# Cross attention with cached keys turned by VectorE's block transpose, and the prompt's keys asked for one head ahead

## The chip, the cores and the metric

The kernel runs on one core of one Trainium2 chip. The metric is the device time of one execution in microseconds. Three runs of the kernel before gave 2087.58, 2092.14 and 2093.4 us (median 2092.14).

## The reference

A two-layer encoder step in fp32 over a prompt of 512 frames and 8 running streams of 16 frames each ("sample"). Each layer is a mixer, a cross attention and a feed-forward block. The change is in the cross attention: 4 heads of 256 dimensions over 256 memory tokens. The sample's keys and values come from a cache, for each stream its own; the prompt's are projected from its memory.

```python
def cross_attn(h, mk, mv, w_q, w_o):
    b, t, _ = h.shape
    q = (h @ w_q).reshape(b, t, X_HEADS, X_HEAD_DIM)
    s = jnp.einsum('bqhd,bkhd->bhqk', q, mk).astype(jnp.float32) * X_SCALE
    p = jax.nn.softmax(s, axis=-1).astype(mv.dtype)
    o = jnp.einsum('bhqk,bkhd->bqhd', p, mv).reshape(b, t, X_WIDTH)
    return o @ w_o

# in the trunk, for each layer i
x = x + cross_attn(rmsnorm(x, g_cross[i]), mem_k[i], mem_v[i], w_x_q[i], w_x_o[i])
```

## The kernel before

The program runs the first mixer (FoX), cross attention, feed-forward, the second mixer (MLA), cross attention and feed-forward, one after the other. Activations lie transposed (features on partitions) as a pair of rounded value and rest, `hT0` and `hT1` (four tiles), for 640 columns: 512 of the prompt and 128 of the sample. A product of two such pairs is three matmuls (hi by hi, hi by lo, lo by hi); weights are loaded as `raw`, ScalarE casts the rounded part `whi` (L150) and VectorE subtracts for the rest `wlo` (L151). `gemm` accumulates in a PSUM tile `mm`; all these matmuls have line L204, and those of the prompt's attention (`mm3`) L218. `evac_split` evicts a PSUM tile as such a pair: ScalarE first (L222, L225 with a scale), then VectorE (L223, L226).

`cross_phase` (L828) does one cross attention. Its parts:

- `q_list(h)`: the query projection of head h, two blocks of 128 dimensions (`dt`) by two halves of 320 columns. The weight's 128 columns are the stationary operand. The prompt's queries go to `qT0`, `qT1`, the sample's, spread over 32-column blocks, to `Qp`.
- `sample_list(pr, bq)`: for a pair of heads and four streams. `keys` loads a key `kr` (128 tokens on partitions, 2 token blocks, 256 dimensions; L941, three keys ahead, four buffers), turns it with four TensorE transposes into PSUM (L956) and copies it to `KT`, on VectorE for even streams (L960), on ScalarE for odd ones (L962). `scores` (L969) fills one PSUM tile for four streams with matmuls of 32 columns, then comes the softmax (reduction L872, exponential L874, reciprocal L344, scaling L345), `trans` (L978, copied to `PTs` by ScalarE, L980), `values` (L992) and `turn` (L1002, to `oTs`).
- `prompt_list(h)`: `load` asks for `kv`, the head's keys and values, from a DRAM buffer; `keys` turns them on TensorE (L891) to `kT0`, `kT1` and casts the values to `v0`, `v1` (one buffer each); then, for two halves of the queries, scores, transposes (L915) and values to `oT0`, `oT1`.
- `out_steps(h)`: the output projection of a head, added to `X` in place by VectorE (L332).

`merge` interleaves three lists evenly, and there are four merges per layer: sample (0,0) with prompt head 0 and the query projection of head 2; sample (0,1) with prompt 1 and q 3; sample (1,0) with prompt 2 and the output of head 0; sample (1,1) with prompt 3 and the output of head 1. The program below is not executed in the written order: a list scheduler puts each engine's instructions in one static order, in which the engine then runs them; all loads of the phase are issued by SyncE's queue in its own such order. The merges of layer 0 lie from about 555 to 681 us, those of layer 1 start near 1499 us.

## Time and profile before

| what | us |
|---|---|
| runs of the kernel before | 2087.58, 2092.14, 2093.4 |
| median | 2092.14 |
| the profiled execution | 2091.71 |
| its span in the trace | 2089.9 |
| TensorE busy in the span | 2034.7 |
| VectorE busy | 1390.8 |
| ScalarE busy | 888.0 |

The span is the profiled execution as the trace has it; 1.8 us of the time lie outside. Busy time of TensorE counts matmuls, whose ends are modelled, so the start of one instruction to the start of the next is the better measure of what an instruction takes up. Loads of stationary operands (PEld) overlap matmuls.

### The profile page before, as it was taken

The page shows a single profiled execution, that of the slowest core. Times are in us where ns is not written, and L with a number is a line of the kernel's source. Part 1 is how long each engine was busy: PE and PEld are TensorE (multiplying, and loading weights), DVE is VectorE, ACT ScalarE, POOL GpSimd, SP SyncE. Part 2 cuts the span into 40 slices and gives each one's busy share as a digit, 9 for nine tenths or more (in the row PEclk, how much of TensorE's full clock was granted, in tenths as well). Part 3 has the DMA queues.
Part 4 walks back from the last instruction along what each step waited for, and adds up shares of the span by engine and source line. Part 5 has one row for each costly group of instructions (what it writes and reads, how often), then busy time and mean ns, then how long its engine had stood idle before and what let it go on. Part 6 is the DMA issues. An engine that isn't in the chain of part 4 may idle for free. (4 is left out here: it accounts for less than half of the span.)

```text
span 2089.9 us, 34810 instructions
## 1 busy us (share of the span) xinstructions
PE 2034.7 (97%) x13629; PEld 1817.9 (87%) x13629; DVE 1390.8 (67%) x2658; ACT 888.0 (42%) x1723; POOL 195.2 (9%) x398
## 2 busy tenths in 40 slices
PE   7999999999999999999999989999999999999998
PEld 7988888777987899999998978887987899999996
DVE  5455555655556896687677567777556896686686
ACT  4434444544443443343344455554443443343342
POOL 1222222210000000000002301101000000000000
PEclk9999999999999999999999999999999999999999
DMA  7565655477464322232222342113463322232221
GB/s 194 119 160 124 148 135 142 146 243 229 151 197 133 100 88 74 81 91 71 81 82 64 96 109 52 53 51 102 149 196 131 101 81 75 80 99 71 81 81 61
DMA packets 334203, 236.37 MB, mean 113 GB/s; under 512 B 99140, under 2 KB 298564, under 8 KB 334040
## 3 DMA queue, kind: packets, MB, share of 16 engines
q1 hardware_dynamic: 334040, 234.15, 38.8%
q8 instruction: 108, 1.77, 0.4%
q14 instruction: 55, 0.45, 0.1%
HBM read 216.90 MB, written 17.21 MB: 112 GB/s over the span
## 5 line engine op out<-in xcount | busy, mean ns | idle before, releaser
L204 PE MATMUL mm<-hT,whi 128*128 128x320 f32 x1744 | 287.5, 311 | 2.9 <-ACT hT L222 2.9
L151 DVE TENSOR_TENSOR wlo<-raw,whi 128x1024 fp32r<-128x1024 f32 (+4 forms) x145 | 169.8, 1174 | 156.5 <-ACT whi L150 116.5
L204 PEld LDWEIGHTS mm<-hT,whi 128*128 128x128 f32 x1744 | 261.0, 188 | 6.8 <-ACT hT L222 4.3
L332 DVE TENSOR_TENSOR X<-mm,X 128x512 f32<-128x512 f32 x270 | 183.5, 687 | 119.7 <-PE mm L204 118.1
L150 ACT CAST whi<-raw 128x1024 fp32r<-128x1024 f32 (+4 forms) x145 | 144.8, 1003 | 146.7 <-PE mm L204 74.9
L204 PE MATMUL mm<-whi,oT 128*128 128x512 f32 x544 | 180.3, 407 | 3.8 <-DVE X L332 2.2
L1136 ACT CAST whi<-tw 128x512 fp32r<-128x512 f32 (+1 forms) x120 | 91.9, 766 | 213.7 <-PE mm L204 127.4
L204 PE MATMUL mm<-whi,aT 128*128 128x512 f32 x560 | 173.0, 390 | 1.2 <-ACT aT L1101 1.2
L204 PE MATMUL mm<-hT,wlo 128*128 128x320 f32 x872 | 156.7, 312 | 0.0
L204 PEld LDWEIGHTS mm<-hT,wlo 128*128 128x128 f32 x872 | 133.3, 188 | 3.3 <-issue 3.2
L232 POOL TENSOR_SCALAR rstd<-ss 128x1 f32<-128x1 f32 x49 | 16.2, 330 | 1265.4 <-ACT hn L230 1261.0
L204 PE MATMUL mm<-s,whi 128*128 128x320 f32 x768 | 128.2, 309 | 0.0
L204 PE MATMUL mm<-whi,hT 128*128 128x256 f32 (+2 forms) x800 | 125.5, 295 | 0.3 <-ACT whi L150 0.3
L204 PEld LDWEIGHTS mm<-whi,aT 128*128 128x128 f32 x560 | 104.4, 188 | 23.5 <-ACT aT L1101 2.0
L204 PEld LDWEIGHTS mm<-whi,oT 128*128 128x128 f32 x544 | 96.7, 189 | 26.2 <-DVE X L332 4.6
L204 PEld LDWEIGHTS mm<-s,whi 128*128 128x128 f32 x768 | 116.6, 188 | 0.0
L1137 DVE TENSOR_TENSOR wlo<-tw,whi 128x512 fp32r<-128x512 f32 (+1 forms) x120 | 103.5, 862 | 19.1 <-ACT whi L1136 17.4
L204 PEld LDWEIGHTS mm<-whi,hT 128*128 128x128 f32 x800 | 109.1, 191 | 3.8 <-issue 1.7
L204 PE MATMUL mm<-wlo,oT 128*128 128x512 f32 x272 | 109.0, 401 | 0.0
L204 PE MATMUL mm<-wlo,aT 128*128 128x512 f32 x280 | 108.8, 389 | 0.0
L1136 ACT CAST whi<-raw 128x1024 fp32r<-128x1024 f32 x44 | 46.3, 1052 | 131.7 <-PE mm L204 71.0
L204 PE MATMUL ps_s<-whi,aT 128*128 128x512 f32 x320 | 98.6, 389 | 0.0
(336 smaller groups left out, 4199.4 us busy)
## 6 DMA issues: line engine op xcount, KB each, us to landing
rawg<-w_ffn_gu SPq DMA_DIRECT2D x80, 512.0 KB, 3.8
raw<-w_ffn_down SPq DMA_DIRECT2D x44, 512.0 KB, 3.7
raw<-w_x_kv SPq DMA_DIRECT2D x32, 512.0 KB, 4.4
kr<-cache_mem_k SPq DMA_DIRECT2D x64, 256.0 KB, 4.8
vr<-cache_mem_v SPq DMA_DIRECT2D x32, 512.0 KB, 6.1
raw<-w_fox_in SPq DMA_DIRECT2D x30, 512.0 KB, 6.5
kr<-cache_fox_k SPq DMA_DIRECT2D x64, 128.0 KB, 5.1
vr<-cache_fox_v SPq DMA_DIRECT2D x16, 512.0 KB, 5.2
```

The source lines that it names most:

```text
L150: A.copy(hi[:, 0:m], raw[:, 0:m])
L151: V.tensor_tensor(lo[:, 0:m], raw[:, 0:m], hi[:, 0:m].bitcast(F32), ALU.subtract)
L204: T.matmul(st["ps"][:, 0:n], lhsT=l, rhs=r, start=(j == 0), stop=(j == m - 1))
L232: G.tensor_scalar(r, ss, EPS, None, ALU.add)
L332: V.tensor_tensor(xs, ps, xs, ALU.add)
L1136: A.copy(hi[:, o:o + m], src)
L1137: V.tensor_tensor(lo[:, o:o + m], src, hi[:, o:o + m].bitcast(F32), ALU.subtract)
```

## The change

The cached keys are no longer turned on TensorE. Each key comes in four DMAs (`fill_keys`), 32 partitions each, one for each 64 of the 256 dimensions: 32 tokens on partitions, 8 token blocks by 64 dimensions. One VectorE instruction (`turn_keys`) turns all 32x32 blocks and writes `KT` without PSUM; it reads every second element, so that a block of 128 partitions holds the even dimensions of a head and the other the odd ones. The queries must have the same split: `q_list` loads a head's 256 weight columns at once (two units of four row blocks, instead of one unit of eight for each 128 columns) and gives TensorE the even or the odd columns as stationary operand, and the prompt's key transposes read every second column, too. The prompt's `kv` of head h+1 is asked for right after the keys of head h were turned, that of head 0 ahead of the first merge.

```diff
@@ -828,7 +828,7 @@
 
     def cross_phase(l, nx, rest):
         w_q, w_o = I["w_x_q"][l], I["w_x_o"][l]
-        mk = I["cache_mem_k"][l].rearrange("b (m p) h d -> p (b m) (h d)", p=P)
+        mk = I["cache_mem_k"][l].rearrange("b (m j) h d -> b j m (h d)", j=32)
         mv = I["cache_mem_v"][l].rearrange("b (m p) h d -> p (b m) (h d)", p=P)
         with tc.tile_pool(name=f"x{l}", bufs=2, reuse_waits="tile") as xp:
             AHEAD = 3
@@ -842,11 +842,15 @@
                 L = []
                 d = {}
 
-                def load(dt):
-                    if dt == 0:
-                        qs_[h] = [xp.tile([P, 2, NP], F32R, tag=f"qT{i}", name=f"qT{i}", bufs=2) for i in range(2)]
-                    c0 = h * XD + dt * P
-                    d[dt] = load_w([(0, P, w_q[:, c0:c0 + P])], per=8)
+                def load():
+                    qs_[h] = [xp.tile([P, 2, NP], F32R, tag=f"qT{i}", name=f"qT{i}", bufs=2) for i in range(2)]
+                    d["w"] = load_w([(0, XD, w_q[:, h * XD:(h + 1) * XD])])
+
+                def ops(dt, half):
+
+                    hs = slice(half * HALF, (half + 1) * HALF)
+                    return [(d["w"].get(wi, k).rearrange("p (n t) -> p t n", t=2)[:, dt], nx.T[ai][:, k, hs])
+                            for wi, ai in PASSES for k in range(KD)]
 
                 def done(ps, dt, half):
                     qT = qs_[h]
@@ -860,12 +864,18 @@
 
                 for half in range(2):
                     for dt in range(2):
-                        if half == 0:
-                            L.append(lambda dt=dt: load(dt))
-                        L += gemm(lambda dt=dt, half=half: ws_ops(d[dt], slice(0, P), nx.T,
-                                                                  slice(half * HALF, (half + 1) * HALF), KD),
-                                  HALF, lambda ps, dt=dt, half=half: done(ps, dt, half), parts=3)
-                return L
+                        L += gemm(lambda dt=dt, half=half: ops(dt, half), HALF,
+                                  lambda ps, dt=dt, half=half: done(ps, dt, half), parts=3)
+                return [load] + L
+
+            def fill_keys(r, src, h):
+
+                for g in range(4):
+                    c0 = h * XD + 64 * g
+                    S.dma_start(r[32 * g:32 * g + 32], src[:, :, c0:c0 + 64])
+
+            def turn_keys(dst, r):
+                V.transpose(dst, r.rearrange("p m (i t) -> p t m i", t=2))
 
             def softmax(pw, sp):
                 nm = small.tile([P, 1], F32, tag="nm", name="nm")
@@ -874,22 +884,26 @@
                 A.activation(pw, sp[:, 0:NMEM], AF.Exp, bias=nm, accum_out=ss)
                 softmax_tail(pw, ss, NMEM)
 
+            kvs = {}
+
+            def load_kv(h):
+                if h < 4:
+                    kv = npool.tile([P, 2, 2, XD], F32, tag="gb", name="kv", bufs=1)
+                    kvs[h] = [kv[:, i] for i in range(2)]
+                    for i in range(2):
+                        S.dma_start(kv[:, i], kvd[l][i].rearrange("(t p) n -> p t n", p=P)[:, :, h * XD:(h + 1) * XD])
+
             def prompt_list(h):
                 d = {}
 
-                def load():
-                    kv = npool.tile([P, 2, 2, XD], F32, tag="gb", name="kv", bufs=1)
-                    d["kv"] = [kv[:, i] for i in range(2)]
-                    for i in range(2):
-                        S.dma_start(kv[:, i], kvd[l][i].rearrange("(t p) n -> p t n", p=P)[:, :, h * XD:(h + 1) * XD])
-
                 def keys():
+                    d["kv"] = kvs.pop(h)
                     d["kT"] = [xp.tile([P, 2, NMEM], F32R, tag=f"kT{i}", name=f"kT{i}", bufs=1) for i in range(2)]
                     pt = psum_t()
                     for dt in range(2):
                         for mt in range(2):
                             T.transpose(out=pt[:, dt * NMEM + mt * P:dt * NMEM + (mt + 1) * P],
-                                        in_=d["kv"][0][:, mt, dt * P:(dt + 1) * P], identity=ident)
+                                        in_=d["kv"][0][:, mt].rearrange("p (n t) -> p t n", t=2)[:, dt], identity=ident)
                     evac_split(d["kT"][0], d["kT"][1], pt.rearrange("p (d m) -> p d m", m=NMEM))
                     d["v"] = [xp.tile([P, 2, XD], F32R, tag=f"v{i}", name=f"v{i}", bufs=1) for i in range(2)]
                     evac_split(d["v"][0], d["v"][1], d["kv"][1])
@@ -925,7 +939,7 @@
                     oc = slice(q2 * 256, (q2 + 1) * 256)
                     evac_split(oTp[h][0][:, :, oc], oTp[h][1][:, :, oc], op.rearrange("p (d q) -> p d q", q=256))
 
-                L = [load, keys]
+                L = [keys, lambda: load_kv(h + 1)]
                 for q2 in range(2):
                     L += [lambda q2=q2: scores(q2), trans, lambda q2=q2: values(q2)]
                 return L
@@ -936,9 +950,8 @@
 
                 if n < 32:
                     pr, bq, hh, b = n // 16, n // 8 % 2, n // 4 % 2, n % 4
-                    hc = slice((2 * pr + hh) * XD, (2 * pr + hh + 1) * XD)
-                    krs[n] = xp.tile([P, 2, XD], F32, tag="kr", name="kr", bufs=4)
-                    S.dma_start(krs[n], mk[:, 2 * (4 * bq + b):2 * (4 * bq + b) + 2, hc])
+                    krs[n] = xp.tile([P, 8, 64], F32, tag="kr", name="kr", bufs=4)
+                    fill_keys(krs[n], mk[4 * bq + b], 2 * pr + hh)
 
             def sample_list(pr, bq):
                 Q = Qps[pr]
@@ -947,19 +960,9 @@
                 def keys(hh, b):
                     n = 16 * pr + 8 * bq + 4 * hh + b
                     load_key(n + AHEAD)
-                    kr = krs.pop(n)
                     if b % 2 == 0:
                         d["KT"][hh, b // 2] = xp.tile([P, 2, 2, NMEM], F32, tag="KT", name="KT", bufs=4)
-                    pt = psum_t()
-                    for dt in range(2):
-                        for mt in range(2):
-                            T.transpose(out=pt[:, dt * NMEM + mt * P:dt * NMEM + (mt + 1) * P],
-                                        in_=kr[:, mt, dt * P:(dt + 1) * P], identity=ident)
-                    src = pt.rearrange("p (d m) -> p d m", m=NMEM)
-                    if b % 2 == 0:
-                        V.tensor_copy(d["KT"][hh, b // 2][:, 0], src)
-                    else:
-                        A.copy(d["KT"][hh, b // 2][:, 1], src)
+                    turn_keys(d["KT"][hh, b // 2][:, b % 2], krs.pop(n))
 
                 def scores():
                     sp = psum_s()
@@ -1030,8 +1033,9 @@
             for n in range(AHEAD):
                 load_key(n)
             ql = q_list(0)
-            for f in ql[:6] + rest[:1] + ql[6:8] + rest[1:] + ql[8:] + q_list(1):
+            for f in ql[:5] + rest[:1] + ql[5:7] + rest[1:] + ql[7:] + q_list(1):
                 f()
+            load_kv(0)
             merge(sample_list(0, 0), prompt_list(0), q_list(2))
             merge(sample_list(0, 1), prompt_list(1), q_list(3))
             merge(sample_list(1, 0), prompt_list(2), out_steps(0))
```

The scheduler's order changes with it, in the cross phases alone. The first place is the end of merge 0 on TensorE: from the last sample scores to the sample's values. `mm_6786` and `mm_6773` are the last query projection of the merge, `ps_s_6752` and `ps_s_6748` the sample's scores, `pws` its softmax, `vr` its values. The kernel before:

```order
L969 MATMUL ps_s_6752<-KT_6651,Qp0_6193 32x256 x2
L915 MATMUL ps_t_6779<-cst_79,hn_6710 128x128 x4
L204 MATMUL mm_6786<-hT00_6090,whi_6606 128x320 x4
L204 MATMUL mm_6786<-hT01_6091,whi_6606 128x320 x4
L204 MATMUL mm_6786<-hT10_6092,whi_6606 128x320 x4
L204 MATMUL mm_6786<-hT11_6093,whi_6606 128x320
L978 MATMUL ps_t_6795<-cst_79,pws_6769 128x128 x2
L204 MATMUL mm_6786<-hT11_6093,whi_6606 128x320 x3
L204 MATMUL mm_6786<-hT00_6090,wlo_6607 128x320
L992 MATMUL ps_o_6808<-vr_6611,PTs_6798 32x256 x2
```

In the changed kernel, at the same place on the same engine:

```order
L204 MATMUL mm_6773<-hT11_6093,whi_6508 128x320 x4
L204 MATMUL mm_6773<-hT00_6090,wlo_6503 128x320 x4
L204 MATMUL mm_6773<-hT01_6091,wlo_6509 128x320 x4
L972 MATMUL ps_s_6748<-KT_6664,Qp0_6193 32x256
L972 MATMUL ps_s_6748<-KT_6582,Qp0_6193 32x256 x2
L972 MATMUL ps_s_6748<-KT_6664,Qp0_6193 32x256 x2
L981 MATMUL ps_t_6791<-cst_79,pws_6765 128x128 x2
L995 MATMUL ps_o_6804<-vr_6613,PTs_6794 32x256 x2
L995 MATMUL ps_o_6804<-vr_6647,PTs_6794 32x256 x2
```

The projection's matmuls stood between the scores, the softmax's transposes (L978) and the values (L992); now they stand ahead of the last scores, and the transposes (L981) and values (L995) follow one on the other.

The second place is the border of merge 0 and merge 1 on TensorE, from the last values of the prompt (`ps_o`) on; `kr` is a cached key, `mm_6894` the next merge's projection, `kT0`, `kT1` the prompt's next keys. The kernel before:

```order
L218 MATMUL ps_o_6827<-PT0_6777,v1_6544 128x256
L204 MATMUL mm_6786<-hT01_6091,wlo_6607 128x320 x2
L1002 MATMUL ps_t_6853<-cst_79,osb_6825 128x128 x4
L956 MATMUL ps_t_6869<-cst_79,kr_6622 128x128 x4
L204 MATMUL mm_6894<-hT00_6090,whi_6878 128x320 x4
L204 MATMUL mm_6894<-hT01_6091,whi_6878 128x320 x4
L204 MATMUL mm_6894<-hT10_6092,whi_6878 128x320 x4
```

In the changed kernel, at the same place on the same engine:

```order
L218 MATMUL ps_o_6823<-PT0_6782,v1_6523 128x256
L1005 MATMUL ps_t_6849<-cst_79,osb_6821 128x128 x4
L905 MATMUL ps_t_6885<-cst_79,kv_6550 128x128 x4
L218 MATMUL ps_s_6955<-kT0_6883,qT0_6365 128x256
L218 MATMUL ps_s_6969<-kT0_6883,qT0_6365 128x256
L218 MATMUL ps_s_6955<-kT1_6884,qT0_6365 128x256
L218 MATMUL ps_s_6955<-kT0_6883,qT1_6366 128x256
```

The next projection stood behind the output's transposes (L1002) and one key; now the prompt's keys (L905) follow the output's transposes (L1005), and their scores come at once.

The third place is the same end of merge 0 on VectorE; `qT1` is the eviction of the query projection, `nm` the softmax's maximum, `KT_6664` the last pair of keys of the merge. The kernel before:

```order
L151 TENSOR_TENSOR wlo_6993<-raw_6991,whi_6992 128x1024
L872 TENSOR_REDUCE nm_6770<-ps_s_6752 128x1
L223 TENSOR_TENSOR PT1_6778<-ps_t_6779,PT0_6777 128x512
L344 RECIPROCAL rc_6774<-ssum_6772 128x1
L345 TENSOR_SCALAR pws_6769<-pws_6769,rc_6774 128x256
L151 TENSOR_TENSOR wlo_7259<-raw_7257,whi_7258 128x1024
L223 TENSOR_TENSOR oT1_6548<-ps_o_6827,oT0_6547 128x2x256
L226 SCALAR_TENSOR_TENSOR qT1_6490<-mm_6786,qT0_6489 128x192
```

In the changed kernel, at the same place on the same engine:

```order
L878 STREAM_TRANSPOSE KT_6664<-kr_6561 128x512
L223 TENSOR_TENSOR PT1_6783<-ps_t_6784,PT0_6782 128x512
L226 SCALAR_TENSOR_TENSOR qT1_6500<-mm_6773,qT0_6499 128x192
L878 STREAM_TRANSPOSE KT_6664<-kr_6577 128x512
L882 TENSOR_REDUCE nm_6766<-ps_s_6748 128x1
L344 RECIPROCAL rc_6770<-ssum_6768 128x1
L345 TENSOR_SCALAR pws_6765<-pws_6765,rc_6770 128x256
```

The eviction of the last projection (`mm_6786`) stood behind the softmax's steps; now that of `mm_6773` stands ahead of the last block transpose and the softmax's maximum.

## Rows read from the trace of the kernel before

**Rows 1.** Page, part 1: busy us, share of span, instructions.

```profile
PE 2034.7 (97%) x13629; PEld 1817.9 (87%) x13629; DVE 1390.8 (67%) x2658; ACT 888.0 (42%) x1723; POOL 195.2 (9%) x398
```

**Rows 2.** Table by stretch: length, busy us, clock, DMA share, GB/s.

```profile
616.00:651.00 35.00, 34.84 (x255) 27.90 (x255) 23.15 (x44) 13.61 (x31) 0.00 (x0) 1.00 0.59 190
```

**Rows 3.** Timeline, TensorE: start us, us, engine, line, operation.

```profile
643.71 0.41 PE L978 MATMUL ps_t<-cst,pws 128*128 128x128 f32 x2
...
644.75 1.93 PE L992 MATMUL ps_o<-vr,PTs 128*32 128x256 f32 x32
...
649.53 0.60 PE L956 MATMUL ps_t<-cst,kr 128*128 128x128 f32 x4
649.89 0.71 PE L204 MATMUL mm<-whi,oT 128*128 128x512 f32 x2
```

**Rows 4.** Groups by line, program: busy us, mean ns, idle before.

```profile
L956 PEld LDWEIGHTS ps_t<-cst,kr 128*128 128x128 f32 x256 | 30.0, 140 | 6.1 <-DMA kr<-cache_mem_k 2.2 <-ACT KT L962 1.6 <-DVE KT L960 0.4
...
L960 DVE COPY KT<-ps_t 128x512 f32<-128x512 f32 x32 | 22.0, 688 | 8.1 <-PE ps_t L956 8.1
L692 DVE STREAM_TRANSPOSE KT<-kr 128x512 f32<-128x512 f32 x32 | 21.6, 693 | 0.0
```

**Rows 5.** Groups by line, layer 0's merges (555 to 681): softmax.

```profile
L872 DVE TENSOR_REDUCE nm<-ps_s 128x1 f32<-128x256 f32 x20 | 8.5, 423 | 8.7 <-PE ps_s L218 6.5 <-PE ps_s L969 2.1
...
L344 DVE RECIPROCAL rc<-ssum 128x1 f32<-128x1 f32 x20 | 3.1, 158 | 1.2 <-ACT hn L874 1.2
...
L874 ACT ACTIVATE pws<-ps_s,nm 128x256 f32<-128x256 f32 x4 | 1.9, 481 | 0.0
...
L345 DVE TENSOR_SCALAR pws<-pws,rc 128x256 f32<-128x256 f32 x4 | 1.4, 349 | 0.1
L874 ACT ACTIVATION_READ_ACCUMULATOR pws<-ps_s,nm 128x1 f32 x4 | 0.8, 204 | 0.0
```

**Rows 6.** Groups by line, same stretch: evictions of the projections.

```profile
L332 DVE TENSOR_TENSOR X<-mm,X 128x512 f32<-128x512 f32 x21 | 14.5, 688 | 6.8 <-PE mm L204 6.6
...
L226 DVE SCALAR_TENSOR_TENSOR qT<-mm,qT 128x192 fp32r<-128x192 f32 (+1 forms) x10 | 3.8, 404 | 0.0
...
L225 ACT ACTIVATE qT<-mm 128x192 fp32r<-128x192 f32 (+1 forms) x9 | 3.2, 381 | 0.1
```

**Rows 7.** Timeline of ScalarE after a merge's last values.

```profile
649.17 0.62 ACT L222 CAST v<-kv 128x512 fp32r<-128x512 f32 x1 [1.84 <-PE ps_o L218]
649.70 0.58 ACT L222 CAST oT<-ps_o 128x512 fp32r<-128x512 f32 x1
650.17 0.27 ACT L222 CAST oTs<-ps_t 128x128 fp32r<-128x128 f32 x1
```

**Rows 8.** Groups by line, 555 to 681: the prompt's keys.

```profile
L223 DVE TENSOR_TENSOR kT<-ps_t,kT 128x512 fp32r<-128x512 f32 x4 | 2.8, 692 | 3.4 <-ACT kT L222 3.4
...
L222 ACT CAST kT<-ps_t 128x512 fp32r<-128x512 f32 x4 | 2.3, 586 | 4.5 <-PE ps_t L891 4.5
```

**Rows 9.** Groups by line, 555 to 681: idle weight loads.

```profile
L992 PEld LDWEIGHTS ps_o<-vr,PTs 128*32 128x32 f32 x128 | 3.8, 109 | 3.2 <-ACT PTs L980 1.1
...
L978 PEld LDWEIGHTS ps_t<-cst,pws 128*128 128x128 f32 x8 | 0.8, 140 | 1.4 <-PE mm L204 0.8 <-issue 0.7
```

**Rows 10.** Page, part 5: the projections' weight loads.

```profile
L204 PEld LDWEIGHTS mm<-hT,whi 128*128 128x128 f32 x1744 | 261.0, 188 | 6.8 <-ACT hT L222 4.3
```

**Rows 11.** Timeline, TensorE: a piece of the query projection.

```profile
588.04 2.15 PE L204 MATMUL mm<-hT,whi 128*128 128x320 f32 x13
```

**Rows 12.** The key tile: issues, ns min/median/max.

```profile
L941 SPq DMA_DIRECT2D kr<-cache_mem_k x64: 367/368/679, 515.2 to 1594.9; - x64
```

**Rows 13.** Page, part 6: KB each, median us to landing.

```profile
kr<-cache_mem_k SPq DMA_DIRECT2D x64, 256.0 KB, 4.8
vr<-cache_mem_v SPq DMA_DIRECT2D x32, 512.0 KB, 6.1
...
kr<-cache_fox_k SPq DMA_DIRECT2D x64, 128.0 KB, 5.1
```

## The prediction

> **What bounds the kernel now.** I read the page's busy table first. TensorE is busy in 97% of the span and VectorE in 67% [rows 1]; the next question is whether that also holds where the change acts. The change touches only the cross attention, whose work on cached keys lies in four merges per layer. The table by stretch, read for one of these merges, shows TensorE busy for 34.84 of 35 us at a granted clock of 1.00, VectorE for 23.15 us, the DMA engines at 0.59 [rows 2]. So within a merge TensorE's in-order queue sets the end: an instruction taken out of it shortens the merge by its pitch, and an instruction in it that has to wait lengthens the merge by the wait. Elsewhere the order of every engine stays as it was; there I expect no change.
>
> The timeline of TensorE shows why its queue has no holes now. The sample's two softmax transposes start at 643.71, the values that need them start at 644.75, and the copy of the transposes lies beneath projection matmuls put between the two [rows 3]. The same holds for the scores, the key evictions and the prompt's softmax: each wait has matmuls of the projection in front of it.
>
> **What the change removes.** 256 transposes leave TensorE, four per key. A key's four start at 649.53 and the next matmul starts at 649.89, 0.36 us later [rows 3], so 64 keys are worth 64 x 0.36 = 23 us. Their weight loads waited 6.1 us in the whole program, for key DMAs and key copies [rows 4]; that goes too. At the places where new waits will stand there are small waits already: weight loads of the values and of the softmax transposes sat idle for 3.2 and 1.4 us in one layer's merges [rows 9], some 5 us, or 10 for both layers; since the new waits take their place I count them as gone (bounds 0 and 10, as part of that idle time lies beside running matmuls). Together 23 + 6 + 10 = 39 us, at least 23.
>
> **VectorE.** It loses 32 copies of 0.688 us (22 us) and gains 64 block transposes. The nearest row is the first mixer's block transpose of the same size, 693 ns [rows 4], read without a step; the new one reads every second element. I take 0.69 us: 44 us, so 22 us more, 2.8 per merge. In that merge it makes 23.15 + 2.8 of 35 us: not the bound by itself. If the step doubled it, it would be 8 x 0.69 = 5.5 us per merge more, of which only the transposes at the end of a merge are waited for (below); half of that stands in the upper end.
>
> **What moves: the end of every merge.** This is the term that decides. In the new order the last projection gemm runs in one piece and the sample's tail stands behind it; nothing is left between the links. On TensorE: last gemm, last scores, the two transposes of the softmax, values of the sample, values of the prompt, transposes of the output, of the prompt's keys, and the next prompt's scores. On VectorE the last block transposes stand behind the eviction of that last gemm. Each link, per merge:
>
> (T) Last gemm to last scores. In merge 0: eviction on ScalarE about 0.34 and on VectorE 0.35 (means 0.381 and 0.404 over two widths, the last piece being the narrow one), then one block transpose of 0.69, and some 0.1 for each of three handovers: 1.7 us. In merge 1 two block transposes follow: 2.4. In merges 2 and 3 the eviction is the addition to X of 0.688 [rows 6] and two transposes follow: 2.4. Per layer 1.7 + 3 x 2.4 = 8.9.
>
> (B) Scores to softmax transposes: reduction 0.42, exponential 0.48 with its accumulator read 0.20, reciprocal 0.16, scaling 0.35 [rows 5], with handovers 0.4: 2.0 us, four times 8.0.
>
> (C) Softmax transposes to values: from 643.71 to 644.75 it takes 1.04 us [rows 3], of which the two transposes themselves are some 0.2: 0.8, four times about 3.
>
> (V) The last of the four value loads. It is issued after a key load that waits for the second-last block transpose, in merges 1 and 2. Landing takes 6.1 us [rows 13] and the work from there to its use some 5.4: 0.5 to 2.6 late; as the load's issues are spread, I take 1.0, twice: 2.
>
> (D) Before the next prompt's scores. ScalarE casts v 0.62, oT 0.58, oTs 0.27 and only then kT 0.59, all after the prompt's values end; TensorE has eight transposes, 0.8 to 0.9 us, for that time. ScalarE's starts are 0.5 apart [rows 7]: kT is there about 2.1 after the values, 1.2 after the transposes; VectorE's part, 0.69 [rows 8], then holds the third score matmul for some 0.6 more: 1.85, in merges 0, 1 and 2: 5.5.
>
> (E) The first prompt softmax and the next weights, which now arrive at the start of a merge instead of a merge ahead: a softmax of 1.6 [rows 5], less some 0.75 of scores beside it, is 0.85, three times, and 0.5 in the last, with 0.65 between the first two heads: 3.7.
>
> The sum is 8.9 + 8.0 + 3 + 2 + 5.5 + 3.7 = 31 per layer, 62 for two, against a gain of 39. Bounds: 45 if the handovers vanish and V and E are covered; 80 if V is 2.6 and each block transpose is half as long again.
>
> **Loads that move.** Each key becomes four DMAs of 32 partitions: 256 issues of 0.368 us in place of 64, 192 x 0.368 = 71 us more on the sync queue [rows 12] over eight merges, 9 per merge of some 31. Its queue has waits to spend. The first mixer loads its keys in just this form and they land in about the time of the others, 5.1 against 4.8 us [rows 13]. With three keys asked for ahead and one key used in some 3.9 us I cost this at nothing; the cover is those 11 us. The prompt's k and v load one head ahead is at nothing too: it replaces a wait that the old order already covered. The Trainium skill, "DMA: Bandwidth & Descriptors", Specifications, says that transfers below 512 B miss line rate; a key's runs here fall from 1 KB to 256 B, which speaks against this change. No run here shows runs of 256 B, and the fox keys with runs of 128 B land in 5.1 us; by the page late keys (below) would be likelier, by the row they are not.
>
> **Strided weights.** 768 projection matmuls now read their stationary operand with a step of two. Nothing in the trace does that. A contiguous load lasts 188 ns [rows 10], and 13 matmuls of 320 columns take 2.15 us with the last one's tail, some 0.15 each [rows 11], so there is little slack; at no cost 0, and at twice the pitch of the short transposes (0.36/4 = 0.09, thus 0.2 against 0.15) 768 x 0.05 = 40 us, at most 55. I take 0: loads of 188 ns at a pitch of 0.15 already overlap each other, so that a load alone doesn't set the pitch. The Trainium skill, "SBUF — State Buffer", Door 1: The DMA port swizzle, states that SBUF is read in lines of 16 bytes and that two hits in a line keep full bandwidth: a step of two fp32 still has two. No run here shows it.
>
> **The sum.** The profiled execution took 2091.7 us, 0.4 below the median of the three runs, so they stand for each other. 2091.7 - 39 + 62 = 2115. About 0.3%, 6 us, is what a measurement of this kernel can tell from no change.
>
> **Rivals.**
> - *Slower, the tails as above* (0.56): 2115, from 2098 (stalls of 45) to 2135 (stalls of 80).
> - *Faster: only the softmax is exposed* (0.13). If the chains T, D and E find their inputs earlier than I think, B and C alone remain, 2 x 11 = 22: 2091.7 - 39 + 22 = 2075, or 2065 if C is covered as well. It decides where the stalls fall below 33. For it: TensorE's 97% says that every removed instruction pays. Against it: T stands in the order, not in an estimate.
> - *No change* (0.12): T and B alone decide, 2 x 17 = 34, or the gain is only 23 with half the stalls: 2087 to 2097.
> - *Late keys* (0.12): four issues per key and four times the packets make each merge wait for one key, some 3.9 us, eight times: 2115 + 31 = 2146. For it: the DMA share of 0.59 in merges. Against it: the fox keys.
> - *Strided weight loads cost* (0.07): 2115 + 40 to 55 = 2155 to 2170.
>
> **How the numbers follow.** The likeliest gives 2115. Faster by over 0.3%: 0.13. Within: 0.12. Slower: 0.56 + 0.12 + 0.07 = 0.75. The range from 2078 to 2150 leaves out about half of the faster case, the strided loads and parts of the late keys, near 2 in 10.
>
> **What would show it.** In the profile after: TensorE's busy share in the merges falls to near 85%; idle time before the sample's scores released by VectorE's block transpose, before the softmax transposes by the scaling, before the values by ScalarE's copy, before the prompt's scores by kT, in the sizes above. The block transpose's mean should be 0.69, the pitch of the 320-column matmuls in the query projection 0.15, and key DMAs should release nearly nothing. Wrong would be: merges shorter by some 5 us each (the order's chain is then hidden), a pitch of 0.2 in the projection, or waits of TensorE or VectorE on key DMAs.

## The result, and the profile after

The changed kernel takes 2127.74 us (median of four runs, 2126.04 to 2131.19) against 2090.42 for the kernel before on the same chip: a ratio of 1.0176, 95% interval 1.0159 to 1.0193, so 37 us slower. Its profiled span is 2125.1 us. The first line of the page, to be held against [rows 1] (busy us, share of the span, instructions):

```profile
PE 2030.1 (96%) x13373; PEld 1799.3 (85%) x13373; DVE 1408.9 (66%) x2690; ACT 868.6 (41%) x1691; POOL 197.2 (9%) x398
```

TensorE has 256 matmuls fewer (its transposes count as such) and is busy for only 4.6 us less, in a span that is 35 us longer. The timeline of TensorE at the end of merge 0 shows where it stands still. Columns: start us, us, line, operation, out<-in, count, and in brackets the idle time ahead with what ended it.

```profile
576.75 1.33 PE L204 MATMUL mm<-hT,wlo 128*128 128x320 f32 x8
579.52 1.05 PE L972 MATMUL ps_s<-KT,Qp 128*32 128x256 f32 x10 [1.43 <-DVE KT L878]
582.36 0.41 PE L981 MATMUL ps_t<-cst,pws 128*128 128x128 f32 x2 [1.79 <-DVE pws L345]
583.23 3.47 PE L995 MATMUL ps_o<-vr,PTs 128*32 128x256 f32 x32 [0.46 <-ACT PTs L983]
587.42 1.71 PE L218 MATMUL ps_o<-PT,v 128*128 128x256 f32 x12 [0.71 <-ACT osb L1000]
...
590.85 0.50 PE L218 MATMUL ps_s<-kT,qT 128*128 128x256 f32 x2 [0.81 <-ACT kT L222]
591.84 1.46 PE L218 MATMUL ps_s<-kT,qT 128*128 128x256 f32 x10 [0.48 <-DVE kT L223]
...
595.50 0.30 PE L929 MATMUL ps_t<-cst,hn 128*128 128x128 f32 x1 [0.44 <-DVE hn L345]
```

Read the brackets from above: 1.43 us until the last block transpose (link T of the prediction), 1.79 until the softmax is scaled (B), 0.46 until PTs is copied (C), 0.71 until osb is copied, 0.81 and 0.48 until the prompt's keys are there (D), 0.44 for the prompt's softmax (E): 6.1 us in all, at links that had matmuls of the projections between them before (for another merge in [rows 3]). And the sample's 32 value matmuls take 3.47 us where [rows 3] has 1.93. In the other merges of the layer:

```profile
619.26 2.66 PE L995 MATMUL ps_o<-vr,PTs 128*32 128x256 f32 x32 [0.46 <-ACT PTs L983]
...
654.22 3.36 PE L995 MATMUL ps_o<-vr,PTs 128*32 128x256 f32 x32 [0.46 <-ACT PTs L983]
...
689.88 1.93 PE L995 MATMUL ps_o<-vr,PTs 128*32 128x256 f32 x32 [0.46 <-ACT PTs L983]
```

The wait for the copy is the same, the values' length is not. The table by stretch (busy us of TensorE, weight loads, VectorE, ScalarE, GpSimd; then the granted clock, the share of the DMA engines, GB/s) tells two causes apart:

```profile
583.00:587.00 4.00, 3.47 (x32) 1.39 (x32) 1.02 (x2) 0.40 (x2) 0.00 (x0) 0.57 1.05 312
619.00:622.00 3.00, 2.55 (x32) 1.04 (x32) 1.05 (x2) 0.24 (x2) 0.00 (x0) 1.00 1.08 252
654.00:658.00 4.00, 3.36 (x32) 1.65 (x32) 1.01 (x2) 0.54 (x2) 0.00 (x0) 0.58 1.03 289
...
583.23:619.26 36.03, 29.90 (x226) 24.51 (x226) 17.01 (x38) 11.10 (x28) 0.00 (x0) 0.96 0.58 148
...
1510.00:1660.00 150.00, 127.86 (x870) 100.06 (x869) 79.22 (x161) 43.51 (x103) 0.00 (x0) 0.94 0.57 151
```

In merges 0 and 2 the clock is down to 0.57 and 0.58, near the lower of TensorE's two levels (1.2 of 2.4 GHz), after waits of 1.43, 1.79 and 0.46 us within some 5 us (merge 0); in merge 1 it is 1.00 and the values are 2.66 us long all the same. The same three waits, of 1.40 to 1.43, 1.79 and 0.46 us, stand in all eight merges, and the clock fell in five of them (in layer 1 in merges 0, 1 and 3). What decides between them is not shown.

From one merge's values to the next it takes 36.0, 35.0 and 35.7 us; before, the same rows start at 582.75, 613.04, 644.75 and 674.93, 30.3, 31.7 and 30.2 apart. That is 4.8 us per merge, and the same three intervals of layer 1 give 4.9 (107.8 us in all against 93.2). Eight merges at that rate make 38 us: the loss lies in the merges. TensorE is busy for 29.90 of 36.03 us from the values of merge 0 to those of merge 1, which is 83%; near 85% was forecast.

What answers to [rows 4] and [rows 9], groups by line over the program (busy us, mean ns, idle ahead and what ended it):

```profile
L878 DVE STREAM_TRANSPOSE KT<-kr 128x512 f32<-128x512 f32 x64 | 43.0, 693 | 0.0
...
L972 PE MATMUL ps_s<-KT,Qp 128*32 128x256 f32 x256 | 25.1, 386 | 11.3 <-DVE KT L878 11.3
...
L995 PE MATMUL ps_o<-vr,PTs 128*32 128x256 f32 x256 | 23.5, 494 | 3.8 <-ACT PTs L983 3.7
```

The block transpose with a step of two takes 693 ns, as without a step, and VectorE never waited ahead of one: no key came late.

For the projections' weight loads the row of [rows 10] does not do, since most of its 1744 loads are in other phases and have no step. From 555 to 579 us they are those of the query projection, in the changed kernel and then in the kernel before:

```profile
L204 PEld LDWEIGHTS mm<-hT,whi 128*128 128x128 f32 x64 | 9.6, 196 | 0.8 <-DVE hn L345 0.4 <-issue 0.4
...
L204 PEld LDWEIGHTS mm<-hT,whi 128*128 128x128 f32 x59 | 8.7, 188 | 0.0
```

A load with a step of two takes 196 ns against 188. The pitch of the matmuls hardly moves: 8 matmuls take 1.33 us in the row of 576.75 above, 0.15 each from start to start, as in [rows 11].

### The profile page after: what moved, and what is told of

The parts are those of the page before. It is cut to its first block, busy times and chain, and to the rows that moved or that the text cites. A ratio compares the mean times of both kernels' runs of the same rounds, so it can differ in the third digit from the quotient of the medians.

```text
span 2125.1 us, 34528 instructions
## 1 busy us (share of the span) xinstructions
PE 2030.1 (96%) x13373; PEld 1799.3 (85%) x13373; DVE 1408.9 (66%) x2690; ACT 868.6 (41%) x1691; POOL 197.2 (9%) x398
```

## The experiments

The ratio of each is to the kernel before on the same chip, with its 95% interval; the changed kernel's own is 1.0176. In the edits `...` stands for lines left out.

**One DMA per key (e1).** The key loads alone are undone; all else of the change is kept. The keys' elements then lie in other places than the scores need, so this version is of use for its time alone.

```diff
-        mk = I["cache_mem_k"][l].rearrange("b (m j) h d -> b j m (h d)", j=32)
+        mk = I["cache_mem_k"][l].rearrange("b (m p) h d -> b p m (h d)", p=P)
...
-                for g in range(4):
-                    c0 = h * XD + 64 * g
-                    S.dma_start(r[32 * g:32 * g + 32], src[:, :, c0:c0 + 64])
+                S.dma_start(r.rearrange("p a b -> p (a b)").rearrange("p (m d) -> p m d", m=2), src[:, :, h * XD:(h + 1) * XD])
```

> Everything of the change but the form of the key loads: each cached key comes in one DMA of 1 KB runs instead of four of 256 B runs (the keys' elements then lie in the wrong places, so the sample's scores are not the reference's; the number and size of all VectorE and TensorE instructions stay). The scheduler then puts projection matmuls back between the sample's scores, softmax transposes and values. Theory that the order of the merge's end is the cause: the stalls vanish and the 25 us of TensorE transposes are gained, 2058 to 2072 us. Rival that the block transposes or the strided weights themselves cost: it stays above 2100 us.

2056.69 us, ratio 0.9836 (0.9820 to 0.9852): 35 us faster than before and 71 faster than the changed kernel, with the same number of instructions on TensorE, VectorE and ScalarE. TensorE at the end of merge 0, from its timeline:

```profile
575.34 1.94 PE L970 MATMUL ps_s<-KT,Qp 128*32 128x256 f32 x32
577.20 1.45 PE L204 MATMUL mm<-hT,whi 128*128 128x320 f32 x8
578.48 0.60 PE L927 MATMUL ps_t<-cst,hn 128*128 128x128 f32 x4
578.84 1.27 PE L204 MATMUL mm<-hT,whi 128*128 128x320 f32 x7
579.95 0.38 PE L979 MATMUL ps_t<-cst,pws 128*128 128x128 f32 x2
580.09 0.40 PE L204 MATMUL mm<-hT,whi 128*128 128x320 f32 x1
580.33 0.90 PE L204 MATMUL mm<-hT,wlo 128*128 128x320 f32 x5
581.15 1.93 PE L993 MATMUL ps_o<-vr,PTs 128*32 128x256 f32 x32
```

There is not one bracket. Between the scores (L970) and the softmax transposes (L979) stand 15 projection matmuls, and before the values (L993) six. So the block transposes and the stepped weights, which are all still there, do not make the 71 us. What differs is the key DMAs, for which VectorE never waited in the changed kernel, and the order. That the scheduler changes its order with the form of the loads is seen; what its estimate of such a load is, the runs don't show.

**The form of the key loads alone (e11).** In the kernel before each key comes in four DMAs; TensorE turns it as ever. Here, too, the elements lie in other places than the scores need.

```diff
-                    S.dma_start(krs[n], mk[:, 2 * (4 * bq + b):2 * (4 * bq + b) + 2, hc])
+                    r = krs[n].rearrange("p a (m c) -> p (a m) c", c=64)
+                    for g in range(4):
+                        c0 = (2 * pr + hh) * XD + 64 * g
+                        S.dma_start(r[32 * g:32 * g + 32], mk[4 * bq + b][:, :, c0:c0 + 64])
```

> The kernel before with the form of the key loads alone changed: four DMAs of 32 partitions and 256 B runs per key, turned by TensorE as before (elements lie in the wrong places, so the sample's scores are not the reference's). The scheduler then puts two thirds of the sample's last scores and the key transposes without projection matmuls between them at the end of a merge. Theory that the form of the loads brings the bad order, with or without block transposes: 2110 to 2140 us. Rival that the order is bad only together with VectorE's transposes: 2087 to 2097 us.

2169.77 us, ratio 1.0356 (1.0329 to 1.0384), worse than the theory's 2140: the copies of the turned keys are now waited for as well. A row of TensorE's timeline in merge 0, and groups by line in layer 0's merges:

```profile
589.09 0.41 PE L980 MATMUL ps_t<-cst,pws 128*128 128x128 f32 x2
...
L958 PE MATMUL ps_t<-cst,kr 128*128 128x128 f32 x116 | 17.8, 277 | 4.0 <-DVE KT L962 4.0
L971 PE MATMUL ps_s<-KT,Qp 128*32 128x256 f32 x128 | 15.9, 387 | 5.7 <-DVE KT L962 3.8 <-ACT KT L964 1.4 <-ACT hn L874 0.5
```

The waits end nearly all with VectorE's and ScalarE's copies of keys, none with a DMA. So the four loads per key bring a bad order without any block transpose. It is not the changed kernel's order, though: in merges 0 and 1 the softmax transposes have projection matmuls ahead of them and no wait (the row of 589.09), and in merges 2 and 3 they wait 1.79 us. These 10 us per layer are a part of the loss of 76; the rest was not added up.

**The two other parts alone (e9).** The kernel before with the stepped weights of a whole head and the prompt's keys asked for ahead, cached keys in one DMA and turned by TensorE. The edit is against the changed kernel.

```diff
-            def fill_keys(r, src, h):
...
-            def turn_keys(dst, r):
-                V.transpose(dst, r.rearrange("p m (i t) -> p t m i", t=2))
...
+                    S.dma_start(krs[n], mk[:, 2 * (4 * bq + b):2 * (4 * bq + b) + 2, hc])
...
+                            T.transpose(out=pt[:, dt * NMEM + mt * P:dt * NMEM + (mt + 1) * P],
+                                        in_=kr[:, mt].rearrange("p (n t) -> p t n", t=2)[:, dt], identity=ident)
```

> The kernel before with the two other parts of the change alone: a head's weights loaded at once and read with a step of two (the prompt's and the cached keys, too, in TensorE's transposes), and the prompt's keys and values asked for one head ahead; cached keys are loaded in one DMA and turned by TensorE. Theory that the loss comes with the new form of the key loads alone: within 0.4% of before, 2084 to 2098 us. Rival that the stepped weights or the request ahead cost: 2100 us or more.

2096.71 us, ratio 1.0015 (1.0004 to 1.0025): the theory holds, this version costs some 3 us (1 to 5). One row (a group by line) shows a price of the step that I had not expected:

```profile
L961 PEld LDWEIGHTS ps_t<-cst,kr 128*128 128x128 f32 x256 | 36.5, 206 | 5.2 <-ACT hn L875 1.1 <-ACT KT L967 1.1 <-issue 0.8
```

A transpose's load with a step of two takes 206 ns against 140 in [rows 4], and from one transpose's start to the next it takes 0.120 us at the median against 0.109. For 256 transposes that is 2.8 us, about all that e9 costs; in the changed kernel and in e1 TensorE has no transposes of cached keys, and of the prompt's keys 32 with a step.

**Half of the key DMAs from GpSimd (e2).** The layout stays as changed; only who issues is changed.

```diff
-                    S.dma_start(r[32 * g:32 * g + 32], src[:, :, c0:c0 + 64])
+                    (S, G)[g % 2].dma_start(r[32 * g:32 * g + 32], src[:, :, c0:c0 + 64])
```

> The changed kernel with every second of a key's four DMAs issued by GpSimd instead of SyncE; nothing else is changed in the text, the layout is the right one. The scheduler then hides the ends of the merges as in the kernel before, but for a few waits of the values. Theory of the order: 2060 to 2080 us. Rival that 256 B runs and four DMAs per key are themselves too slow, or GpSimd's issues too late: above 2100 us, with TensorE or VectorE waiting for key DMAs.

2068.29 us, ratio 0.9889 (0.9874 to 0.9904). The keys lie as the scores need them, and this version is faster than both kernels, by 24 us (before) and 59 (changed). The runs of 256 B and the four DMAs per key are thus no bound for the time of before. Its timeline of TensorE has the tail in cover and two kinds of waits left, in two of a layer's merges:

```profile
599.24 1.93 PE L972 MATMUL ps_s<-KT,Qp 128*32 128x256 f32 x32
...
603.42 0.38 PE L981 MATMUL ps_t<-cst,pws 128*128 128x128 f32 x2
...
608.49 1.69 PE L218 MATMUL ps_o<-PT,v 128*128 128x256 f32 x12 [0.71 <-ACT osb L1000]
...
612.37 1.20 PE L204 MATMUL mm<-whi,oT 128*128 128x512 f32 x4 [1.26 <-ACT whi L150]
```

The scores have no bracket, nor have the softmax transposes; the copy osb and the next weights' cast are still waited for. In layer 0 they make some 4 us; in layer 1 the prompt's keys are waited for in place of the cast. From e2 to e1 it is 12 us in both layers.

**Only the order (e5).** Projection steps written behind the sample's scores may stand only behind them in TensorE's queue; no load or instruction differs from the changed kernel.

```diff
+            if n == 2 and hold[0] is not None:
+                with tc.issue_after(hold[0]):
+                    lists[n][i]()
...
+                    hold[0] = mm if not hasattr(mm, "ins") else mm.ins
```

> The changed kernel with one thing added: in each merge, the projection steps written behind the sample's scores may only stand behind those scores in TensorE's queue (edges of order, no waits; no instruction or load is added). TensorE then has 8 matmuls (1.2 us) behind the scores and 8 (or 5) before the values; the wait for the last block transposes, for osb and for the prompt's keys stay. Theory of the order, by the stalls measured in the changed kernel: per merge 1.2 of the softmax's 2.2 us, 0.3 of the copy, 1.0 of the clock: 8 x 2.5 = 20 us less, 2100 to 2115 us. Rival that the key loads in their new form bound the merge whatever the order: no change, 2124 us or more.

2119.09 us, ratio 1.0130 (1.0115 to 1.0145), 9 less than the changed kernel, not 20. Its timeline of TensorE tells why:

```profile
581.93 0.41 PE L990 MATMUL ps_t<-cst,pws 128*128 128x128 f32 x2 [0.42 <-DVE pws L353]
...
648.55 1.64 PE L980 MATMUL ps_s<-KT,Qp 128*32 128x256 f32 x12 [2.08 <-DVE KT L886]
```

The wait for the softmax is 0.42 us in merge 0 instead of 1.79, but the last block transposes are waited for 2.08 us in merge 2 instead of 1.40: those matmuls stood ahead of them before. And the clock, which I had counted as won back, still fell in three of the eight merges (0.66 over 613 to 618 us in merge 1). The direction was right; I had not counted what the moved matmuls had covered. So with the very loads of the changed kernel an order by hand gained 9 of the 71 us; that the order makes the rest goes by e1, by e2 and by the sum of the links below.

**A filler for the clock (e4).** 16 transposes of a constant behind the last scores.

```diff
+                    d["last"] = mm.ins if hasattr(mm, "ins") else mm
...
+                    with tc.issue_after(d["last"]):
+                        for i in range(16):
+                            T.transpose(out=pt[:, 2 * P:3 * P], in_=ident, identity=ident)
```

> The changed kernel with 16 useless transposes of a constant on TensorE behind the sample's last scores, where TensorE waits 1.8 us for the softmax; their order is fixed, nothing else moves. Theory that this wait lowers the clock of what follows (the sample's values took 3.5 us in one merge and 1.9 in another): the values take 1.93 us in every merge, 9 us less, 2118 us. Rival that the longer values are late loads: no change, 2126 to 2130 us.

2120.75 us, ratio 1.0140 (1.0124 to 1.0156): 7 us less, though TensorE has 128 instructions more. The values from the timeline, the clock over the merges of layer 1 from the table by stretch, and a group by line over the program:

```profile
584.88 1.93 PE L999 MATMUL ps_o<-vr,PTs 128*32 128x256 f32 x32 [0.46 <-ACT PTs L987]
...
619.29 2.45 PE L999 MATMUL ps_o<-vr,PTs 128*32 128x256 f32 x32 [0.46 <-ACT PTs L987]
...
653.99 2.60 PE L999 MATMUL ps_o<-vr,PTs 128*32 128x256 f32 x32 [0.46 <-ACT PTs L987]
```

```profile
1510.00:1655.00 145.00, 129.50 (x937) 103.94 (x936) 81.41 (x163) 42.23 (x102) 0.00 (x0) 1.00 0.60 158
```

```profile
L999 PEld LDWEIGHTS ps_o<-vr,PTs 128*32 128x32 f32 x256 | 7.9, 109 | 11.8 <-ACT PTs L987 5.6 <-DMA vr<-cache_mem_v 2.0
```

The clock stays at 1.00 in the merges of both layers, where the changed kernel has 0.94 in layer 1. The values take 1.93 us in merges 0 and 3, but 2.45 and 2.60 in 1 and 2, where the prediction had the fourth value load late: 0.5 and 0.7 us remain of that link, and weight loads of the values do wait for a value's DMA (2.0 us in the program). The rest of the long values in merges 0 and 2 was the clock; in merge 1, where the clock had not fallen, 0.2 us remain open.

**Block transposes twice (e12).**

```diff
-                V.transpose(dst, r.rearrange("p m (i t) -> p t m i", t=2))
+                for _ in range(2):
+                    V.transpose(dst, r.rearrange("p m (i t) -> p t m i", t=2))
```

> The changed kernel with every block transpose done twice over the same data (44 us more of VectorE work, 5.5 us per merge); TensorE's order stays. Theory that only the transposes at the end of a merge are waited for: 0.69 more in merge 0 and 1.4 in the others of a layer, 10 us, and some more at the border, where the next keys' transposes stand ahead of the prompt's keys: 2138 to 2148 us, with idle times of 2.1 us (now 1.4) before the last scores. Rival that VectorE itself bounds the merges: 2160 us or more.

2157.36 us, ratio 1.0313 (1.0296 to 1.0330): 30 us more than the changed kernel, between the two theories. Groups by line over the program, to be held against those of the changed kernel above:

```profile
L973 PE MATMUL ps_s<-KT,Qp 128*32 128x256 f32 x256 | 31.3, 440 | 21.5 <-DVE KT L879 21.5
...
L996 PE MATMUL ps_o<-vr,PTs 128*32 128x256 f32 x256 | 27.8, 608 | 3.7 <-ACT PTs L984 3.7
```

```profile
582.00:587.00 5.00, 2.40 (x12) 0.80 (x12) 2.47 (x6) 0.89 (x3) 0.00 (x0) 0.57 0.48 120
```

The waits ahead of the last scores grew from 11.3 to 21.5 us, the 10 of the first theory. The matmuls behind them became slower, 440 against 386 and 608 against 494 ns in the mean, at a clock of 0.57 in the row: a longer wait costs again in what follows it. Over layer 0's merges the granted clock is 0.87 (555 to 715 us), against 0.98 in the changed kernel (555 to 700). How the other 20 us split between clock and border was not separated.

**The prompt's keys not asked for ahead (e3, e6).** The same edit in the changed kernel and in that of e2.

```diff
-                L = [keys, lambda: load_kv(h + 1)]
+                L = [lambda: load_kv(h), keys]
...
-            load_kv(0)
```

> The changed kernel with the prompt's keys and values asked for in their own merge again, as before the change. The order at the border of two merges then has projection matmuls around the prompt's key transposes again, while the end of the merge stays as in the changed kernel. Theory that asking one head ahead exposed the copy of the prompt's keys: 6 borders x (0.81 + 0.48 + some 0.3) = about 10 us less than the changed kernel, 2113 to 2122 us. Rival that the early request pays: 2128 us or more.

> The kernel with half of the key DMAs issued by GpSimd (2068 us), with the prompt's keys and values asked for in their own merge, as before the change. Theory that the request ahead has little worth of its own and that the 23 us it was worth in the changed kernel lay in the order at the border, where matmuls waited for their weights: 2064 to 2076 us. Rival that it hides a load: 2085 to 2095 us.

e3 takes 2150.38 us, ratio 1.0284 (1.0267 to 1.0302), 23 more than the changed kernel: my theory fell. TensorE at the border of merges 0 and 1:

```profile
588.31 2.93 PE L218 MATMUL ps_o<-PT,v 128*128 128x256 f32 x12 [0.71 <-ACT osb L1000]
...
594.08 0.88 PE L204 MATMUL mm<-hT,whi 128*128 128x320 f32 x4 [1.99 <-ACT whi L150]
```

```profile
588.00:594.00 6.00, 3.78 (x16) 3.38 (x16) 1.77 (x4) 2.29 (x6) 0.00 (x0) 0.67 0.94 160
```

The projection now stands ahead of the prompt's keys, and its weights are cast too late: one wait of 1.99 us takes the place of 0.81 and 0.48, and at a clock of 0.67 the prompt's values ahead of it take 2.93 us (1.71 in the changed kernel). In e6 the order is a good one and the edit is worth nothing: 2069.82 us, ratio 0.9894 (0.9879 to 0.9909), against 0.9889. So in e2's order the request ahead has no worth of its own; the 23 us that it was worth in the changed kernel came with the order.

**Three tries to better e2 (e7, e8, e10).** Value loads issued by ScalarE (e7), and the sample's values in the scores' PSUM buffers, with that (e8) and without it (e10). The edit of e8 and e10 moves the values of one attention in each of the two mixers (L733, L1680) to those buffers as well.

```diff
-                    S.dma_start(v, mv[:, 8 * bq + 4 * b2:8 * bq + 4 * b2 + 4, hc])
+                    A.dma_start(v, mv[:, 8 * bq + 4 * b2:8 * bq + 4 * b2 + 4, hc])
...
                 def values():
-                    op = psum_o()
+                    op = psum_s()
```

> As the kernel with half of the key DMAs on GpSimd, and the cached values' loads issued by ScalarE. The scheduler then puts more projection matmuls between the prompt's values and the sample's, and around the border. Theory of the order: the waits left there (0.7 us for the copy osb in two merges, 1.3 for weights in two) go, 8 us per program: 2058 to 2064 us, near the 2057 of the kernel with single key DMAs. Rival that issuing on ScalarE delays its copies: 2070 us or more.

> As the kernel on three queues, with the sample's values in the scores' two PSUM buffers, so that the prompt's values need not wait for their copy. Theory: no wait of the prompt's values for that copy is left, 2056 to 2063 us. Rival that the scores then wait for the buffer: 2066 us or more.

> The kernel with half of the key DMAs on GpSimd (2068 us), with the sample's values in the scores' two PSUM buffers. Theory that the prompt's values wait 0.7 us for the copy osb since both use one buffer, and lose some 1.1 us by it in two merges per layer: 4 us less, 2062 to 2066 us. Rival that the wait goes elsewhere: 2067 us or more.

2072.31, 2075.94 and 2073.11 us, ratios 0.9907 (0.9892 to 0.9921), 0.9919 (0.9903 to 0.9936) and 0.9896 (0.9876 to 0.9917): none is better than e2, all three theories failed, and each time lies in the range of the rival. In e7 keys do come late, as the group of the block transposes shows (program), and TensorE waits for an eviction that stands behind one of them on VectorE, ahead of the merges (timeline):

```profile
L878 DVE STREAM_TRANSPOSE KT<-kr 128x512 f32<-128x512 f32 x64 | 44.4, 701 | 24.3 <-DMA kr<-cache_mem_k 12.9 <-issue 11.2 <-PE ps_s L972 0.2
...
542.51 2.50 PE L204 MATMUL mm<-hT,whi 128*128 128x320 f32 x8 [4.54 <-DVE hT L223]
```

The copies of ScalarE, which e7's rival named, were not looked at. In e10 the wait for osb has gone from the prompt's values to the output's transposes, the next user of that copy (timeline):

```profile
612.00 0.66 PE L1005 MATMUL ps_t<-cst,osb 128*128 128x128 f32 x4 [0.80 <-ACT osb L1000]
```

From the first output transposes of layer 0 to its last, e10 takes what e2 takes (85.0 and 85.1 us by the timelines), and in layer 1 nearly so (87.0 and 86.7): in the merges the edit neither won nor lost. What the moved values of the mixers cost was not separated.

## Why the prediction was right, and where its sizes were off

The direction, the mechanism and its places came out as forecast: 2115 was said for 2127.7, in the range. That it came so near owes something to luck, since two links that were left out and three that were too large partly cancel. By its steps:

- **The gain, 39 us.** With all chains in cover, e1 gains 35 us on the kernel before, the stepped weights and the request ahead included. The 3 us of e9 need not be added to that: they are about what its stepped transposes of cached keys cost, which e1 does not have. The term was some 4 too large; counting all 10 us of small waits as gone is the likeliest excess, which no run shows.
- **The stalls, 62 us.** The changed kernel and e1 differ by 71 us, and only in their key DMAs and the order. For the links I added up, over layer 0's merges in the timeline, each matmul's time to the start of the next beyond the usual pitch of its shape, less the same in the kernel before (idle times in brackets are shorter, since they count from a matmul's modelled end). Per layer: T 9.3 us (8.9 was said), B 8.7 (8.0), D 5.5 (5.5): the large terms were right. C is 1.2 (3); E is 1.5 (3.7); V is 1.2 (2), with e4's clock.
- **Two links were left out, and they make most of the miss.** The prompt's values wait for the copy osb, 0.7 us by the bracket and 3.4 per layer by these sums, since both products use one PSUM buffer; before, projection matmuls stood in between. And the clock: I had priced the stalls at the full clock, although they put several us of waits in a row. It costs 7 us by the filler. The two make 7 + 7 = 14 us; what C, E and V were too large by is 2 x (1.8 + 2.2 + 0.8) = 10; T and B were 2 too small. That leaves 6 of the 9 us between 62 and 71 told; the other 3 were not looked for. With the 4 of the gain they are the 13 us by which 23 (62 less 39) fell short of 36 (71 less 35; the measured loss is 37).
- **Loads at nothing.** True as to landing: VectorE never waited for a key, and late keys, the rival, did not occur. The request ahead is worth nothing in e2's order either (e6). But the sentence missed what the loads do: the order changes with their form, by e1 and e11. I had taken the new order as given and not asked which part of the change brought it.
- **Strided weights at nothing.** True for the projections as far as the pitch goes: loads of 196 against 188 ns at a pitch of 0.15 us either way, and e1, with them, is fast. By the Trainium skill, "SBUF — State Buffer", Door 1: The DMA port swizzle, a step of two fp32 keeps full bandwidth; the projections' loads come near to that, but the row of e9 differs for the load of a transpose, 206 against 140 ns, and the measurement decides.
- **Runs of 256 B.** The rule of "DMA: Bandwidth & Descriptors" in the Trainium skill, Specifications, on transfers under 512 B gave late keys a chance. No run here tells the rate of such runs by itself. The median landing of a 64 KB piece, 3.6 us, is shorter than the 4.8 of a whole key before, though a key is there only with the last of its four pieces; no block transpose of the changed kernel waited for one, and e2 is faster than before with the same runs:

```profile
kr<-cache_mem_k SPq DMA_DIRECT2D x256, 64.0 KB, 3.6
```

- **The faster rival** needed stalls below 33 us. By what parts the changed kernel from e1 they are 71 us.

## What to carry to other kernels

Where a scheduler sets the order, a change in one place (here the form of a load that no engine waits for) can move every chain that hid behind other work; compare the order before the durations, and find the part that brings it by building each part alone. Price an exposed chain link by link, with each copy that shares a buffer, and add the clock: waits in a row can slow the matmuls that follow them. And when a bad order comes with a good idea, look for another way to issue the same loads before the idea is dropped.

## What was not expected of the hardware

- Waits of 1.43, 1.79 and 0.46 us, with 1.05 and 0.41 us of matmuls between them, were followed by a clock of 0.57 over the next 4 us; so it was, or nearly, in five of eight merges, while the same waits left it at 1.00 in three. With 16 useless transposes in the second wait it stayed at 1.00 in all, and the kernel was 7 us faster.
- A transpose's weight load in fp32 took 206 ns with a step of two and 140 without, a projection's load 196 against 188; VectorE's block transpose of 128x512 took 693 ns with and without the step.
- A DMA issue on GpSimd is not free, but it fitted: in e2 128 issues took 0.59 us in the mean, and the kernel was faster than before:

```profile
L875 POOL DMA_DIRECT2D kr<-cache_mem_k x128 | 75.3, 590 | 165.1 <-DVE KT L878 55.7 <-issue 46.7 <-DMA kr<-cache_mem_k 29.0
```
